# One layer on two batches on one core: which engine makes the low parts, and in what order the last parts are added

## The chip, the cores and the metric

The kernel runs on one core of a Trainium2 chip. The metric is the device time in microseconds (us) of one execution. The engines are TensorE (PE, matmuls), VectorE (DVE), ScalarE (ACT) and GpSimd (POOL), each of which runs its own instructions in order; SyncE (SP) issues the DMAs, in order too. On PE a weight load (PEld) goes ahead of each matmul.

## What is computed

One encoder layer with a final norm, with the same weights, for a batch `x_sample` of 512 tokens and a batch `x_prompt` of 1024 tokens, with 1024 channels, all in float32:

```python
def encoder_layer(x, ...):
    h = rmsnorm(x, g_attn)
    proj = h @ w_in                              # q, k, v of two mixers and the gates
    ...
    a = dilated_mixture(qa, ka, va, rel_bias)    # 3 groups of 4 heads
    a = a.reshape(b, s, A_OUT_WIDTH) @ w_a_out
    bo = window_gqa(qb, kb, vb, rel_bias, sink)  # 8 query heads
    bo = bo @ w_b_out
    g_a, g_b = jnp.split(jax.nn.sigmoid(gates + b_gate), 2, axis=-1)
    x = x + (g_a * a + g_b * bo) @ w_o
    u = dwconv(rmsnorm(x, g_ffn) @ w_up, conv_w, conv_b)
    u_gate, u_val = jnp.split(u, 2, axis=-1)
    return x + (jax.nn.gelu(u_gate) * u_val) @ w_down   # D_FF = 2816

def trunk(x, ...):
    return rmsnorm(encoder_layer(x, ...), g_final)
```

## The kernel before

**Split operands.** Every matmul operand is split into a high part `hi`, cast by ScalarE to a shorter format, and a low part `lo` = value − `hi`, subtracted by VectorE or GpSimd. A product is the sum of three matmuls, hi·hi, hi·lo and lo·hi. So before PE can use a tile, ScalarE casts it and another engine subtracts; the third matmul needs the subtraction. `wload` (L123) does this for weights: a DMA into `raw`, the cast to `whi` (L138), the subtraction to `wlo` (L141), every third weight on VectorE and the others on GpSimd.

**Stages.** The sample runs first: norm, projections and attention, `merge`, `ffn`. In the middle of its `ffn` (after channel tiles 11 and 15) the prompt's norm is mixed in. Then the prompt: attention, `merge`, an up-projection with fewer products (`up_strassen`), and `down`.

**Branch inputs.** `merge` first makes six split inputs `ab` with `branch_in` (L715), two for mixer A, four for mixer B: loads of an attention output `bo` and of a factor row `bf`, their product on VectorE (L730), for mixer A the sum of three of them (L732), the cast `abhi` (L735), the subtraction `ablo` on GpSimd (L736). `bo` and `bf` lie in a pool of as many buffers as there are row tiles (4 in the sample, 8 in the prompt).

**Merge.** For each of 8 channel tiles `j`: the two branches' matmuls into `psa`, multiplied into the gates `sg` on VectorE (L803), added on GpSimd (L806), cast to `mhi` (L807), subtracted to `mlo` on GpSimd (L808). The split tile and its rows of `w_o` form a part. `accumulate` (L822) adds parts to the residual: for each job, that is 128 tokens by 512 channels, three matmuls for each part into one PSUM bank `pacc`, then one addition to `xacc` on VectorE (L835). The last group of the sample has parts 6 and 7, and 8 jobs; that of the prompt parts 6 and 7, and 16 jobs.

**ffn of the sample.** For each of 22 channel tiles `i`, two up-projections with their convs (L861 to L864), GELU, the gated product `y` (L878), its cast `ghi` (L881) and its subtraction `glo` on GpSimd (L882), which with the rows of `w_down` form a part. Every second tile two parts are accumulated. At the end parts 20 and 21 are left; 8 jobs share a pool of four banks. For the first four jobs part 20 goes into four banks with an addition each, then part 21 with another four; for the last four jobs both parts go into one bank.

**down of the prompt.** For each half of the tokens and each of 22 parts `k`, `prepare` (L1102) loads a piece `graw` of the gated product and the weight rows `wraw` into a pool of 6 buffers and splits them with `ring_split` (L986 on) into three pairs of `rhi` and `rlo`, out of a ring of 7 buffers each. Eight banks hold the sums of 4 row tiles by 2 halves of the channels. Parts go one after the other over all banks, but in the second half the last two parts go row tile by row tile: 12 matmuls, then two additions to `xres` (L1154), the final norm, and the output `yo` (L1118), which is stored.

**Order.** Programs of the engines are not in the order of the source: a scheduler places the instructions of each engine in an order of its own by the dependences, so the rows of the order are shown with the change.

## Time and profile before

| | |
|---|---|
| median of three runs | 2279.0 us (2277.1, 2279.0, 2288.47) |
| profiled execution | 2286.05 us |
| its span, first to last instruction | 2284.2 us |
| mean granted clock of PE | 0.983 |
| PE busy | 2189.2 us, 96% of the span |
| VectorE busy | 1273.4 us, 56% |
| ScalarE busy | 1016.6 us, 45% |
| GpSimd busy | 573.7 us, 25% |
| chain that ended last | PE 75%, VectorE 5%, GpSimd 3%, ScalarE 3%, issue 2%, DMA 1% |

The three runs give the time; the profiled execution is one more, with its own time, and all rows come from it. A share of the chain says which engine's work the end of the program goes back to. The granted clock is the share of full speed, 2.4 GHz, that PE's matmuls had; 0.50 is 1.2 GHz.

### The profile page before, as it was taken

To read this page: it belongs to the slowest core of one execution; us is meant where nothing else is said; L and a number is where in the kernel's file an instruction comes from. 1 tells how busy PE (TensorE), PEld (TensorE's weight loads), DVE (VectorE), ACT (ScalarE), POOL (GpSimd) and SP (SyncE) were. 2 spreads that over 40 slices of the span, in tenths; PEclk is the share of its full clock that TensorE was granted. 3 is DMA by queue.
4 is the path that set the end of the run, shared out by engine and by line. 5 is a ranking of instruction groups with operands and counts; after the bars stand their busy time and mean duration, and the time that the engine had idled before them with its cause. 6 is when DMAs were issued, how large, how long until landed. Compare 5 with 4: busy or idle time off the path is not lost.

```text
span 2284.2 us, 28441 instructions
## 1 busy us (share of the span) xinstructions
PE 2189.2 (96%) x10627; PEld 1822.3 (80%) x10627; DVE 1273.4 (56%) x2161; ACT 1016.6 (45%) x1878; POOL 573.7 (25%) x322
## 2 busy tenths in 40 slices
PE   7999999899999999999999999998899999999998
PEld 6877777688878888989787788887778888888886
DVE  4547532554464446465577443434978888863534
ACT  5646532433354336565577212124555555543433
POOL 2211154333333310110000423231733333200000
PEclk9999999899999999999999999999999999999999
DMA  5454353333333331324211921112222222254542
GB/s 168 136 159 125 121 154 105 102 101 94 101 121 100 94 97 47 106 78 128 63 41 54 271 61 45 50 44 96 87 67 83 83 83 83 87 212 140 172 155 101
DMA packets 247981, 240.80 MB, mean 105 GB/s; under 512 B 19808, under 2 KB 204848, under 8 KB 247844
## 3 DMA queue, kind: packets, MB, share of 16 engines
q1 hardware_dynamic: 247844, 238.99, 33.6%
q8 instruction: 83, 1.36, 0.2%
q14 instruction: 54, 0.44, 0.1%
HBM read 202.46 MB, written 42.79 MB: 107 GB/s over the span
## 4 chain that ended last, share of the span: by engine, by line
PE 75%; DVE 5%; POOL 3%; ACT 3%; issue 2%; DMA 1%; SPq 0%; DVEq 0%; ACTq 0%; POOLq 0%
PE psuA L984 9%; PE psuC L984 4%; PE pacc L833 4%; PE psg L147 4%; PE psg L149 3%; PE psg L148 3%; PE pacc L1114 3%; PE pacc L1113 3%; PE pacc L1115 3%; PE pacc L832 3%; PE pacc L831 3%; PE psu L148 3%; PE psu L147 3%; PE psu L149 3%; PE psuB L984 2%
## 5 line engine op out<-in xcount | busy, mean ns | idle before, releaser
L141 POOL TENSOR_TENSOR wlo<-raw,whi 128x1024 fp32r<-128x1024 f32 (+1 forms) x120 | 282.5, 2360 | 869.8 <-ACT whi L138 664.2
L138 ACT CAST whi<-raw 128x1024 fp32r<-128x1024 f32 (+1 forms) x178 | 182.3, 1031 | 381.0 <-PE pacc L833 133.5
L835 DVE TENSOR_TENSOR xacc<-xacc,pacc 128x512 f32<-128x512 f32 x236 | 159.1, 687 | 142.8 <-PE pacc L833 142.2
L141 DVE TENSOR_TENSOR wlo<-raw,whi 128x1024 fp32r<-128x1024 f32 (+1 forms) x58 | 72.6, 1251 | 147.6 <-ACT whi L138 147.4
L147 PE MATMUL psg<-hhi,whi 128*128 128x512 f32 x384 | 151.0, 393 | 1.1 <-ACT frow L520 1.1
L148 PE MATMUL psg<-hlo,whi 128*128 128x512 f32 x384 | 150.5, 392 | 0.0
L149 PE MATMUL psg<-hhi,wlo 128*128 128x512 f32 x384 | 150.4, 392 | 0.0
L990 ACT CAST rhi<-rraw 128x512 fp32r<-128x512 f32 x132 | 81.4, 622 | 139.7 <-PE psuA L984 51.0
L147 PE MATMUL psu<-hhi,whi 128*128 128x512 f32 x352 | 137.6, 391 | 0.0
L149 PE MATMUL psu<-hhi,wlo 128*128 128x512 f32 x352 | 137.3, 390 | 0.0
L148 PE MATMUL psu<-hlo,whi 128*128 128x512 f32 x352 | 137.3, 390 | 0.0
L1114 PE MATMUL pacc<-rlo,rhi 128*128 128x512 f32 x352 | 137.2, 390 | 0.0
L1115 PE MATMUL pacc<-rhi,rlo 128*128 128x512 f32 x352 | 136.9, 389 | 0.0
L1113 PE MATMUL pacc<-rhi 128*128 128x512 f32 x352 | 136.8, 389 | 0.0
L991 DVE TENSOR_TENSOR rlo<-wraw,rhi 128x512 fp32r<-128x512 f32 x88 | 57.3, 689 | 133.3 <-ACT rhi L990 133.3
L991 DVE TENSOR_TENSOR rlo<-rraw,rhi 128x512 fp32r<-128x512 f32 x132 | 108.4, 839 | 23.3 <-ACT rhi L990 21.2
L803 DVE TENSOR_TENSOR sg<-sg,psa 128x512 f32<-128x512 f32 x48 | 32.9, 687 | 152.3 <-PE psa L149 127.5
L990 ACT CAST rhi<-wraw 128x512 fp32r<-128x512 f32 x88 | 50.5, 619 | 148.2 <-PE pacc L1115 144.5
L147 PE MATMUL psq<-hhi,whi 128*128 128x512 f32 x240 | 100.3, 418 | 1.2 <-DVE vb L356 0.7
L148 PE MATMUL psq<-hlo,whi 128*128 128x512 f32 x240 | 96.6, 402 | 0.0
L149 PE MATMUL psq<-hhi,wlo 128*128 128x512 f32 x240 | 96.1, 400 | 0.0
L1019 POOL TENSOR_TENSOR rraw<-rraw 128x512 f32<-128x512 f32 x44 | 89.9, 2044 | 15.7 <-DVE rlo L991 12.7
(254 smaller groups left out, 6108.5 us busy)
## 6 DMA issues: line engine op xcount, KB each, us to landing
raw<-in_w_in_dram SPq DMA_DIRECT2D x80, 512.0 KB
raw<-in_w_up_dram SPq DMA_DIRECT2D x44, 512.0 KB
rraw<-in_w_up_dram SPq DMA_DIRECT2D x44, 512.0 KB
wraw<-in_w_down_dram SPq DMA_DIRECT2D x44, 512.0 KB
raw<-in_w_down_dram SPq DMA_DIRECT2D x22, 512.0 KB
gv<-y SPq DMA_DIRECT2D x22, 512.0 KB
graw<-gv SPq DMA_DIRECT2D x44, 256.0 KB
raw<-in_w_o_dram SPq DMA_DIRECT2D x16, 512.0 KB
```

The lines of the kernel that those rows point to most:

```text
L138: nc.scalar.copy(out=hi[:, :n], in_=raw[:, :n])
L141: eng.tensor_tensor(out=lo[:, :n], in0=raw[:, :n], in1=hi[:, :n].bitcast(F32), op=ALU.subtract)
L147: mm(out, whi, r[0], start=start, stop=False)
L148: mm(out, whi, r[1], start=False, stop=False)
L149: mm(out, wlo, r[0], start=False, stop=stop)
L835: nc.vector.tensor_tensor(out=x, in0=x, in1=p, op=ALU.add)
L984: mm(out, a[:, cols], b, start=start and j == 0 and n == 0, stop=j == 3 and n == 2, skip_group_check=True)
L990: nc.scalar.copy(out=hi, in_=src)
L991: nc.vector.tensor_tensor(out=lo, in0=src, in1=hi.bitcast(F32), op=ALU.subtract)
L1113: mm(p, a, whi, start=first, stop=False)
L1114: mm(p, a, wlo, start=False, stop=False)
L1115: mm(p, b, whi, start=False, stop=last)
```

## The change

Five places are edited.

1. `wload`: while a layer has made at most `quick` weights, the subtraction is on VectorE. `quick` is 0, and 4 in the sample, whose first norm stands at the program's start. The third weight was on VectorE already.
2. `branch_in`: all subtractions `ablo` on VectorE.
3. `merge`: for the last channel tile, the sum and the subtraction on VectorE. `accumulate` with `late=True`, used for the last group (in the prompt for its first 8 of 16 jobs): all parts but the last go into the first four banks ahead of the last part's matmuls.
4. `ffn`: for the last channel tile the subtraction on VectorE; part 20 is accumulated for all 8 jobs with an addition each, and then part 21 for all 8 with another: 16 additions where there were 12.
5. `down`: in the second half the last three parts, 19 to 21, go row tile by row tile, 18 matmuls each, and their pieces `ehi` and `elo` have a pool of their own of 9 buffers each, outside of the ring.

Behind the first edit the line numbers grow by one (`branch_in`, `merge`), and at the end by 22.

```diff
     def __init__(self, tc, w, const, dram):
         self.tc, self.nc, self.w, self.c, self.dram = tc, tc.nc, w, const, dram
-        self.loads = 0
+        self.loads = self.quick = 0
...
     def wload(self, srcs, ncols, pool=None):
...
         nc.scalar.copy(out=hi[:, :n], in_=raw[:, :n])
         self.loads += 1
-        eng = nc.vector if self.loads % 3 == 0 else nc.gpsimd
+        eng = nc.vector if self.loads % 3 == 0 or self.loads <= self.quick else nc.gpsimd
         eng.tensor_tensor(out=lo[:, :n], in0=raw[:, :n], in1=hi[:, :n].bitcast(F32), op=ALU.subtract)
         return hi, lo
...
         self.wden = self.ms.tile([P, self.NT, 8], F32, tag="wden", name="wden")
         if rows is not None:
+            self.quick = 4
             turn = vectors[0](self.qk, "qk")
             for tt in range(0, NT, 2):
...
         hi, lo = (ab.tile([P, T], F32R, tag="ab", name=n) for n in ("abhi", "ablo"))
         nc.scalar.copy(out=hi, in_=acc)
-        nc.gpsimd.tensor_tensor(out=lo, in0=acc, in1=hi.bitcast(F32), op=ALU.subtract)
+        nc.vector.tensor_tensor(out=lo, in0=acc, in1=hi.bitcast(F32), op=ALU.subtract)
         return hi, lo
...
             for hf, cols in enumerate(halves):
                 t = sg[0][hf]
-                nc.gpsimd.tensor_tensor(out=t, in0=t, in1=sg[1][hf], op=ALU.add)
+                eng = nc.vector if j == KT - 1 else nc.gpsimd
+                eng.tensor_tensor(out=t, in0=t, in1=sg[1][hf], op=ALU.add)
                 nc.scalar.copy(out=mhi[:, cols], in_=t)
-                nc.gpsimd.tensor_tensor(out=mlo[:, cols], in0=t, in1=mhi[:, cols].bitcast(F32), op=ALU.subtract)
+                eng.tensor_tensor(out=mlo[:, cols], in0=t, in1=mhi[:, cols].bitcast(F32), op=ALU.subtract)
             merged.append((mhi, mlo, wo))
         if norm is None:
-            self.accumulate(merged, pw, "w")
+            self.accumulate(merged, pw, "w", late=True)
             return
         del self.h
-        self.accumulate(merged, pw, "w", range(0, 4))
+        self.accumulate(merged, pw, "w", range(0, 4), late=True)
         norm = norm(ps, "m")
         next(norm)
...
         return norm
...
-    def accumulate(self, parts, psum, tag, tiles=None):
+    def accumulate(self, parts, psum, tag, tiles=None, late=False):
         nc = self.nc
         mm = nc.tensor.matmul
-        for tt in tiles or range(self.NT):
-            for nh in range(2):
-                cols = slice(nh * 512, nh * 512 + 512)
-                p = psum.tile([P, 512], F32, tag=tag, name="pacc")
-                for i, (hi, lo, (whi, wlo)) in enumerate(parts):
-                    a, b = hi[:, tt * P:(tt + 1) * P], lo[:, tt * P:(tt + 1) * P]
-                    mm(p, a, whi[:, cols], start=i == 0, stop=False)
-                    mm(p, a, wlo[:, cols], start=False, stop=False)
-                    mm(p, b, whi[:, cols], start=False, stop=i == len(parts) - 1)
-                x = self.x[tt][:, cols]
-                nc.vector.tensor_tensor(out=x, in0=x, in1=p, op=ALU.add)
+        def add(p, i, tt, cols):
+            hi, lo, (whi, wlo) = parts[i]
+            a, b = hi[:, tt * P:(tt + 1) * P], lo[:, tt * P:(tt + 1) * P]
+            mm(p, a, whi[:, cols], start=i == 0, stop=False)
+            mm(p, a, wlo[:, cols], start=False, stop=False)
+            mm(p, b, whi[:, cols], start=False, stop=i == len(parts) - 1)
+        jobs = [(tt, slice(nh * 512, nh * 512 + 512)) for tt in tiles or range(self.NT) for nh in range(2)]
+        early = [psum.tile([P, 512], F32, tag=tag, name="pacc") for _ in jobs[:4]] if late else []
+        for p, job in zip(early, jobs):
+            for i in range(len(parts) - 1):
+                add(p, i, *job)
+        for n, (tt, cols) in enumerate(jobs):
+            p = early[n] if n < len(early) else psum.tile([P, 512], F32, tag=tag, name="pacc")
+            for i in range(len(parts) - 1 if n < len(early) else 0, len(parts)):
+                add(p, i, tt, cols)
+            x = self.x[tt][:, cols]
+            nc.vector.tensor_tensor(out=x, in0=x, in1=p, op=ALU.add)
...
     def ffn(self, ctx, hooks, xnp):
...
             lo = gvp.tile([P, T], F32R, tag="glo", name="glo")
             nc.scalar.copy(out=hi, in_=yv)
-            nc.gpsimd.tensor_tensor(out=lo, in0=yv, in1=hi.bitcast(F32), op=ALU.subtract)
+            eng = nc.vector if i == FT - 1 else nc.gpsimd
+            eng.tensor_tensor(out=lo, in0=yv, in1=hi.bitcast(F32), op=ALU.subtract)
             parts.append((hi, lo, self.wload([W["w_down"][i * P:(i + 1) * P, :]], D, wdp)))
             if i in hooks:
                 hooks[i](dn, "d")
             if i == FT - 1:
-                first = range(NT // 2)
-                self.accumulate(parts[:-1], dn, "d", first)
-                self.accumulate(parts[-1:], dn, "d", first)
+                self.accumulate(parts[:-1], dn, "d")
             if i == FT - 2:
                 gf = xnp.tile([P, D], F32, tag=xtag, name="gf")
                 nc.sync.dma_start(gf, bass.AP(tensor=c["g_final"].tensor, offset=c["g_final"].offset,
                                               ap=[[0, P], [1, D]]))
-        self.accumulate(parts, dn, "d", range(NT // 2, NT))
+        self.accumulate(parts[-1:], dn, "d")
         for tt in range(NT):
             y = xnp.tile([P, D], F32, tag=xtag, name="yo")
...
         xp, yo, sm = pool("xres", 8), pool("yo", 4), pool("dsm", 4)
         W = self.w
+        end = pool("end", 9)
         gf = pool("gf", 1).tile([P, D], F32, name="gf")
         gsrc = self.c["g_final"]
         nc.sync.dma_start(gf, bass.AP(tensor=gsrc.tensor, offset=gsrc.offset, ap=[[0, P], [1, D]]))
...
+        def split(src, last):
+            if not last:
+                return self.ring_split(src)
+            hi, lo = (end.tile([P, 512], F32R, tag=f"e{s}", name=f"e{s}") for s in ("hi", "lo"))
+            nc.scalar.copy(out=hi, in_=src)
+            nc.vector.tensor_tensor(out=lo, in0=src, in1=hi.bitcast(F32), op=ALU.subtract)
+            return hi, lo
         def prepare(half, k):
+            last = half == 1 and k >= FT - 3
             graw = self.rraw.tile([P, 512], F32, tag="rraw", name="graw")
             nc.sync.dma_start(graw, self.gv_d[k][:, half * 512:half * 512 + 512])
             wraw = self.rraw.tile([P, D], F32, tag="rraw", name="wraw")
             nc.sync.dma_start(wraw, W["w_down"][k * P:(k + 1) * P, :])
-            return self.ring_split(graw), [self.ring_split(wraw[:, nh * 512:nh * 512 + 512]) for nh in range(2)]
+            return split(graw, last), [split(wraw[:, nh * 512:nh * 512 + 512], last) for nh in range(2)]
...
         def add(w, p, tt, nh, first, last):
...
                 for tt, x in enumerate(xs):
                     nc.sync.dma_start(x, self.x_d[half * 4 + tt])
-            if half == 1 and k == FT - 2:
+            if half == 1 and k >= FT - 3:
                 continue
-            if half == 0 or k < FT - 2:
+            if half == 0 or k < FT - 3:
                 w = ready.pop(0)
                 for tt in range(4):
...
             y = yo.tile([P, D], F32, tag="y", name="yo")
             for nh, cols in enumerate(halves):
-                for i in range(2):
-                    add(ready[i], acc[tt, nh], tt, nh, False, i == 1)
+                for i in range(3):
+                    add(ready[i], acc[tt, nh], tt, nh, False, i == 2)
                 nc.vector.tensor_tensor(out=x[:, cols], in0=x[:, cols], in1=acc[tt, nh], op=ALU.add)
             rs, = self.rstd([x], sm, lambda: y, 2)
...
```

The order of the instructions at three places:

VectorE (DVE) at the sample's last down-projection, before; `y` is the conv's output and then the gated product, `xacc` the residual:

```order
L862 SCALAR_TENSOR_TENSOR y<-psu,vecs,y 128x511
L835 TENSOR_TENSOR xacc<-xacc,pacc 128x512
L864 SCALAR_TENSOR_TENSOR y<-psu,vecs,y 128x511
L835 TENSOR_TENSOR xacc<-xacc,pacc 128x512
L878 TENSOR_TENSOR y<-y 128x512
L835 TENSOR_TENSOR xacc<-xacc,pacc 128x512 x6
L184 RECIPROCAL rs<-rs 128x1
```

and after:

```order
L847 TENSOR_TENSOR xacc<-xacc,pacc 128x512
L876 SCALAR_TENSOR_TENSOR y<-psu,vecs,y 128x511
L847 TENSOR_TENSOR xacc<-xacc,pacc 128x512
L890 TENSOR_TENSOR y<-y 128x512
L847 TENSOR_TENSOR xacc<-xacc,pacc 128x512 x2
L895 TENSOR_TENSOR glo<-y,ghi 128x512
L847 TENSOR_TENSOR xacc<-xacc,pacc 128x512 x11
L184 RECIPROCAL rs<-rs 128x1
```

`glo` of part 21, which GpSimd made, now stands among the additions, and eight additions of each kind (part 20, part 21) stand where six pairs and a joint sum stood.

TensorE (PE) at the same place, before, with numbers since the names differ by them; `whi_6568` is the weight of part 20 and `whi_6652` that of part 21:

```order
L831 MATMUL pacc_6672<-whi_6568,ghi_6563 128x512
L832 MATMUL pacc_6672<-wlo_6569,ghi_6563 128x512
L833 MATMUL pacc_6672<-whi_6568,glo_6564 128x512
L831 MATMUL pacc_6677<-whi_6652,ghi_6647 128x512
L832 MATMUL pacc_6677<-wlo_6653,ghi_6647 128x512
L833 MATMUL pacc_6677<-whi_6652,glo_6648 128x512
```

and after, the same six places:

```order
L833 MATMUL pacc_6672<-whi_6568,ghi_6563 128x512
L834 MATMUL pacc_6672<-wlo_6569,ghi_6563 128x512
L835 MATMUL pacc_6672<-whi_6568,glo_6564 128x512
L833 MATMUL pacc_6677<-whi_6568,ghi_6563 128x512
L834 MATMUL pacc_6677<-wlo_6569,ghi_6563 128x512
L835 MATMUL pacc_6677<-whi_6568,glo_6564 128x512
```

Behind the fourth bank (`pacc_6672`) the next four banks of part 20 follow, where part 21 stood; part 21 begins twelve matmuls later.

VectorE at the prompt's branch inputs, before; `bo` is a branch output times its factor `bf`, `ablo` its low part:

```order
L730 TENSOR_TENSOR bo<-bo,bf 128x1024 x2
L732 TENSOR_TENSOR bo<-bo 128x1024
L141 TENSOR_TENSOR wlo<-raw,whi 128x1024
L730 TENSOR_TENSOR bo<-bo,bf 128x1024
L732 TENSOR_TENSOR bo<-bo 128x1024
L730 TENSOR_TENSOR bo<-bo,bf 128x1024 x2
L803 TENSOR_TENSOR sg<-sg,psa 128x512 x2
L730 TENSOR_TENSOR bo<-bo,bf 128x1024 x2
L803 TENSOR_TENSOR sg<-sg,psa 128x512 x2
```

and after:

```order
L731 TENSOR_TENSOR bo<-bo,bf 128x1024
L733 TENSOR_TENSOR bo<-bo 128x1024
L737 TENSOR_TENSOR ablo<-bo,abhi 128x1024
L731 TENSOR_TENSOR bo<-bo,bf 128x1024
L737 TENSOR_TENSOR ablo<-bo,abhi 128x1024
L731 TENSOR_TENSOR bo<-bo,bf 128x1024
L804 TENSOR_TENSOR sg<-sg,psa 128x512 x2
L737 TENSOR_TENSOR ablo<-bo,abhi 128x1024
L731 TENSOR_TENSOR bo<-bo,bf 128x1024
L737 TENSOR_TENSOR ablo<-bo,abhi 128x1024
L731 TENSOR_TENSOR bo<-bo,bf 128x1024
L737 TENSOR_TENSOR ablo<-bo,abhi 128x1024
```

A subtraction follows each product, and the one of the fourth input stands behind two gate products (`sg`).

ScalarE (ACT) at the prompt's last weights, before:

```order
L990 CAST rhi<-graw 128x512
L990 CAST rhi<-wraw 128x512 x2
L990 CAST rhi<-graw 128x512
L990 CAST rhi<-wraw 128x512 x2
L179 ACTIVATE yo,ms<-xres 128x512
```

and after; `ehi` are the pieces of parts 19 to 21:

```order
L1119 CAST ehi<-graw 128x512
L1119 CAST ehi<-wraw 128x512
L1001 CAST rhi<-wraw 128x512 x2
L1001 CAST rhi<-graw 128x512
L1119 CAST ehi<-wraw 128x512
L1119 CAST ehi<-graw 128x512
L1119 CAST ehi<-wraw 128x512 x2
L1119 CAST ehi<-graw 128x512
L1001 CAST rhi<-wraw 128x512 x2
L1119 CAST ehi<-wraw 128x512 x2
L179 ACTIVATE yo,ms<-xres 128x512
```

The casts of parts 19 to 21 stand among, and in part ahead of, those of parts 17 and 18.

## Rows read from the trace of the kernel before

**Rows 1.** PE's waits over the span: what waited for what, us in total, times, longest

```profile
PE pacc L831 <- ACT ghi L881: 4.7, 2, 3.6
PE psa L148 <- POOL ablo L736: 4.1, 4, 1.7
PE pacc L833 <- POOL mlo L808: 3.3, 5, 1.2
PE psv L305 <- POOL wlo L141: 1.6, 1, 1.6
```

**Rows 2.** windows: length, busy us (count) of PE, PEld, DVE, ACT, POOL; PEclk; DMA

```profile
297.60:301.00 3.40, 3.40 (x10) 2.63 (x9) 0.37 (x1) 0.42 (x1) 1.28 (x1) 0.50 0.62 218
813.10:819.80 6.70, 6.08 (x13) 4.29 (x14) 2.64 (x5) 2.45 (x4) 1.27 (x1) 0.50 0.01 2
819.90:825.30 5.40, 5.36 (x24) 4.07 (x22) 4.41 (x14) 3.40 (x8) 0.00 (x0) 1.00 0.00 0
```

**Rows 3.** timeline at the sample's last down-projection: start, us, engine, line, instruction, idle before

```profile
812.81 0.68 DVE L835 TENSOR_TENSOR xacc<-xacc,pacc 128x512 f32<-128x512 f32 x1
812.93 0.62 ACT L881 CAST ghi<-y 128x512 fp32r<-128x512 f32 x1 [4.11 <-DVE y L878]
813.60 0.80 PE L831 MATMUL pacc<-whi,ghi 128*128 128x512 f32 x1 [3.64 <-ACT ghi L881]
813.62 1.27 POOL L882 TENSOR_TENSOR glo<-y,ghi 128x512 fp32r<-128x512 f32 x1 [8.48 <-ACT ghi L881]
824.87 0.39 PE L833 MATMUL pacc<-whi,glo 128*128 128x512 f32 x1
```

**Rows 4.** timeline of the sample's branch inputs: PE, POOL, DVE and DMA issues

```profile
292.99 1.56 DVE L730 TENSOR_TENSOR bo<-bo,bf 128x512 f32<-128x512 f32 x1 [2.75 <-DMA bf<-frow]
295.26 0.50 PE L147 MATMUL psa<-abhi,whi 128*128 128x512 f32 x1 [1.23 <-ACT abhi L735]
295.29 1.54 POOL L736 TENSOR_TENSOR ablo<-bo,abhi 128x512 fp32r<-128x512 f32 x1 [1.28 <-ACT abhi L735]
296.85 1.09 SPq L728 DMA_DIRECT2D bf<-frow  x2
296.88 0.50 PE L148 MATMUL psa<-ablo,whi 128*128 128x512 f32 x1 [0.88 <-POOL ablo L736]
300.63 0.69 DVE L730 TENSOR_TENSOR bo<-bo,bf 128x512 f32<-128x512 f32 x1 [3.26 <-DMA bf<-frow]
```

**Rows 5.** timeline of the prompt's branch inputs

```profile
1287.42 1.22 DVE L730 TENSOR_TENSOR bo<-bo,bf 128x1024 f32<-128x1024 f32 x1
1299.12 2.18 ACT L735 CAST abhi<-bo 128x1024 fp32r<-128x1024 f32 x2 [3.59 <-DVE bo L730]
1300.24 2.36 POOL L736 TENSOR_TENSOR ablo<-bo,abhi 128x1024 fp32r<-128x1024 f32 x1 [2.24 <-ACT abhi L735]
1302.66 0.50 PE L148 MATMUL psa<-ablo,whi 128*128 128x512 f32 x1 [1.70 <-POOL ablo L736]
```

**Rows 6.** timeline at the last channel tiles of the two merges

```profile
419.19 2.26 POOL L806 TENSOR_TENSOR sg<-sg 128x512 f32<-128x512 f32 x1
422.15 0.50 PE L831 MATMUL pacc<-whi,mhi 128*128 128x512 f32 x1 [0.98 <-ACT mhi L807]
1566.50 0.50 PE L833 MATMUL pacc<-whi,mlo 128*128 128x512 f32 x1 [0.41 <-POOL mlo L808]
```

**Rows 7.** timeline of the first matmuls

```profile
12.65 2.90 DVE L200 TENSOR_SCALAR xin<-xin,rs 128x1024 f32<-128x1024 f32 x1
12.65 5.13 POOL L141 TENSOR_TENSOR wlo<-raw,whi 128x1024 fp32r<-128x1024 f32 x2 [10.88 <-ACT whi L138]
```

**Rows 8.** timeline of the prompt's last row tiles

```profile
2248.17 0.33 SPq L1106 DMA_DIRECT2D wraw<-in_w_down_dram  x1
2273.80 0.39 PE L1115 MATMUL pacc<-rhi,rlo 128*128 128x512 f32 x1
2279.61 1.42 DVE L1118 SCALAR_TENSOR_TENSOR yo<-xres,rs,gf 128x512 f32<-128x512 f32 x2
```

## The prediction

> **What bounds the kernel now.** I read the busy times first: TensorE (PE) works for 96% of the span, so a change that leaves its matmuls alone can win only where PE stands still or runs at the lower clock. Next I read PE's waits, grouped by what ended them [rows 1]: the last product `ghi` of a group 4.7 us, the branch low parts `ablo` 4.1, the merged low parts `mlo` 3.3, the first weight's low part `wlo` 1.6. That is 13.7 us of 2284, and it is the stock that this change draws on. Last I read the granted clock by windows [rows 2]: right after such waits PE runs at 0.50, the 1.2 GHz level, for 6.7 us at 813.1 and for 3.4 us at 297.6. In the window behind the first of them 24 matmuls take 5.4 us, 0.226 us each. The ten that are recorded in the second stretch would need 2.3 of its 3.4 us, which leaves 1.1 lost; half of its length, by the ratio of the clocks, is 1.7. A few records can be missing from a trace, so I count 1.7.
>
> The sum is made against the profiled execution, 2286.05 us (span 2284.2, so 1.85 us lie outside). The median of the runs is 2279.0, 7 us less, and that gap is not explained by anything below; I carry the difference over to the median.
>
> **Part by part.** Negative is a gain.
>
> *a. Start, three weight halves to VectorE: 0 (−1.5 to +1.5).* PE waits 1.6 us for GpSimd's first `wlo` [rows 1], and the normalising instruction on VectorE takes 2.90 us beside GpSimd's two halves of 5.13 us together [rows 7]. With GpSimd out of the way that instruction should shrink, and the transposes that follow it come sooner. But the first `wlo` now queues on VectorE behind two pairs of `hlo` and a second `xin`: 12.65 plus about 4.5 us, so its matmul starts near 17.2 instead of 15.05, with eight transposes done before it that came after. Idle time about equal.
>
> *b1. Sample, branch inputs: −3.0 (−3.6 to −2.0 if all holds, 0 if a later wait takes it).* The step is a ring: product on VectorE, high part on ScalarE, low part on GpSimd, which frees the buffer for the load of the input after next. The load at 296.85 is issued 0.02 us after the GpSimd subtraction (295.29 + 1.54 = 296.83) ends, and the product at 300.63 waits 3.26 us for it [rows 4]. On VectorE the subtraction costs 0.69, as that product does: 0.85 saved in each turn. So not only PE's wait of 0.88 for `ablo` goes; the wait of 1.23 for `abhi` before it and the load after it move up too. Step by step: inputs 2 and 3 come 0.5 to 0.9 us earlier, the subtraction of input 3 ends near 295.1 instead of 296.83 (a weight half of 1.2 us stands ahead of it on VectorE), its matmul starts near 295.2 instead of 296.88, a gain of 1.7. Less idle time there should leave the clock up: 1.7 more. The load then caps the gain: if it did not move, input 5 would be ready at 302, where PE used it at 304.1, a cap of 2.0; since it moves by 1.7, the cap is 3.6. I take 3.0.
>
> *b2. Prompt, branch inputs: +0.5 (−1 to +3).* Here the subtraction takes 2.36 on GpSimd and would take 1.22 on VectorE [rows 5]. But VectorE now runs product and subtraction in turn, as the rows of the order behind the diff show, and each subtraction waits for ScalarE's cast of 1.09 (2.18 for two). A turn is 1.22 + 1.09 + 1.22 = 3.5 us, and the product of input 5 is queued behind the subtraction of input 4, where before it ran ahead. From 1298.5 on (the subtraction of input 3 now stands behind two gate products) the last `ablo` ends at 1305.6; GpSimd ended it at 1300.24 + 2 × 2.36 = 1304.96. PE waits 1.70 for the first of these two today; that falls, and the last one is later by 0.6. The upper end adds a stretch of low clock like the one in [rows 2].
>
> *c. Sample, last channel tile: −1.4 (−1.4 to −0.4).* GpSimd's addition takes 2.26 us and PE then waits 0.98 for the cast [rows 6], and shortly after another 0.4 for the low part, which is in the `mlo` line of [rows 1]. On VectorE the pair costs 2 × 0.69. "Other parts first" gives nothing here, since the scheduler had issued part 6 ahead of part 7 already.
>
> *d. Prompt, last channel tile: −0.4* for the wait at 1566.50 [rows 6]. Nothing else there waits.
>
> *e. Sample, last down-projection: −4.7 (−5.0 to −2.0).* Before, PE stops after 12 matmuls of part 20, at 813.60 − 3.64 = 809.96, until the cast of part 21 (812.93 + 0.62) has ended, and is done with 36 more at 824.87 + 0.39 = 825.26 [rows 3]: 15.3 us, of which 36 × 0.226 = 8.1 is work at full clock. After, all 24 matmuls of part 20 come first. The 12 extra ones need banks that the four additions free; the last of these ends at 812.81 + 0.68 = 813.49, so PE runs until 814.2 with three short waits of about 0.6. By then `ghi` is there (813.55). `glo` on VectorE costs 0.69 behind one addition, ready near 814.9, against 813.62 + 1.27 = 814.89: equal. PE waits 0.3 for it and does the other 24 by 820.2 at full clock: −5.0. Four more additions, 16 instead of 12, cost 0.69 each on VectorE, at a pace (0.61 from start to start) just below PE's 0.68 for a bank; I take 0.3 for them. If the short waits still bring the low clock, about 3 us come back: −2.0.
>
> *f. Prompt, three token-major rows: −1.3 (−2.4 to 0).* PE ends at 2273.80 + 0.39 = 2274.19 and the last output is computed at 2279.61 + 1.42 = 2281.03 [rows 8]: 6.84 us, because VectorE needs about 3.8 us for a row tile (two additions of 0.69, an output of 1.3, eight small ones) where PE needs 12 × 0.226 = 2.7. With 18 matmuls PE needs 4.1 and VectorE keeps up; what is left is the last tile's own chain and one output ahead of it, 5.5 us.
>
> The moved DMA issues cost nothing by what I can see: the sample's outputs go behind loads of the next stage's bias on SP, and nobody waits for an output; the load of the final gain goes later, and its first use is the prompt's first output.
>
> Sum: 0 − 3.0 + 0.5 − 1.4 − 0.4 − 4.7 − 1.3 = −10.3, so 2275.8 for a profiled execution and **2268.7** for the median.
>
> **A rule against the change.** A VectorE instruction that stood beside GpSimd's weight halves took 2.90 us [rows 7], and a product 1.56 where 0.69 is usual [rows 4]. So moved work is not simply 0.69 wherever GpSimd still splits weights. The Trainium skill, SBUF — State Buffer, section Who interferes with whom, says that a VectorE instruction with two SBUF inputs and a GpSimd instruction that reads SBUF exclude each other, the second waiting for the whole of the first. With that rule both rows agree, and applied to each of three places it gives 2276.4 (rival 3) against the 2268.7 of the sum.
>
> **Rivals.** *1. The clock stays up everywhere.* b1 −3.6, c −1.4, d −0.4, e −5.0, f −2.4, b2 −1: −13.8, 2265.2. For it: both stretches follow idle time that shrinks. Against: PE keeps some waits in each place.
> *2. The low clock stays at the ffn end and in the branch inputs.* e −2.0, b1 −1.7, b2 +0.5, the rest as above: −6.3, 2272.7. For it: after the change PE still stops three or four times around 811 to 815.
> *3. GpSimd blocks the moved work.* A half is 5.13 / 2 = 2.57 us; in three places (start, sample branch inputs, sample merge) a moved instruction waits for a whole one: +7.7, so −2.6, 2276.4. Against: GpSimd loses 22 instructions, and in the prompt's branch inputs it has hardly anything else.
> *4. Slower: the casts of the last rows wait for loads.* ScalarE now casts parts 19 to 21 ahead of the weight of part 18, in order, and these casts wait for loads. A weight is issued at 2248.17 [rows 8] and the DMA engines are quiet by 2251, so 2.9 us. With that, part 18 is split about 1.2 us before PE wants it, and part 21 about 2.4 before. With a landing of L us PE waits (L − 4.1) + (L − 5.3): from L = 9.9 on this passes 10.3 with the low clock's share left out. At L = 11 it gives +12.6 − 10.3 = +2.3, 2281.3. Nothing at this place in the trace is that slow.
>
> **Chances.** Forecast (−8 to −12.5) 0.45; rival 1 0.30; rival 2 0.13; rival 3 0.08; rival 4 0.04. A measurement can tell about 0.5%, 11.4 us: faster than 2267.6 holds rival 1 and the better edge of the forecast, 0.38; slower than 2290.4 asks for L of about 15.6 in rival 4, or for something I do not see, 0.02; same 0.60. The range leaves out the far ends of rivals 1 and 3, and rival 4: 2263 to 2277.
>
> **What would show it.** In the changed profile: PE's wait for `ghi` at the sample's last group falls from 3.6 to under 0.5 and the first matmul of the prompt's values comes 5 us sooner after the group began; no window at 0.50 within 15 us of it (rival 2 if there is). In the sample's branch inputs no wait for `ablo` above 0.3, and the last load issued 1.5 us earlier; in the prompt's a wait for `abhi` above 1 us appears. The end lies 5.5 us behind the last matmul. Any PE wait for `ehi`, `elo` or `rhi` after 2230 is rival 4. I would be wrong if a place that was not edited changes by more than 2 us.

## The result

The changed kernel takes 2269.3 us (median of 7 runs, 2262.4 to 2270.6) against 2279.0 of the kernel before (7 runs, 2276.7 to 2288.5): ratio 0.995, 95% interval 0.9936 to 0.9964, a gain of 8 to 15 us. In a second series, beside a further kernel, it took 2265.7 against 2279.7, ratio 0.9941 (0.9928 to 0.9955). 2268.7 was forecast, with a range of 2263 to 2277.

The profiled execution fell by more, from 2286.05 to 2270.56, because that of before was a long one. So a term must not be read off this pair alone; the experiments below give more profiles of each place with its edit, and for all places but the last down-projection also several without.

**The page after**, part 1, answers to the table of before: GpSimd (POOL) works 51.5 us less, VectorE (DVE) 15.8 more, and PE is busy 8 us less with the same 10,627 matmuls. Up to its last matmul PE stands at 0.50 for 47.8 us where it was 71.7, which fits that. Little of it can be put down to the edits: the eleven other profiles below have 34 to 61 us, and ffn_engine, which is the kernel before with one subtraction moved, has 44.

```profile
PE 2181.1 (96%) x10627; PEld 1815.7 (80%) x10627; DVE 1289.2 (57%) x2187; ACT 1016.4 (45%) x1878; POOL 522.2 (23%) x300
```

**PE's waits over the span** of the changed kernel, as in [rows 1] (what waited for what, us in total, times, longest):

```profile
PE psa L147 <- ACT abhi L736: 4.6, 4, 1.5
PE pacc L835 <- POOL mlo L810: 3.2, 3, 1.2
PE psa L148 <- DVE ablo L737: 1.3, 3, 0.5
PE pacc L833 <- ACT ghi L893: 1.0, 1, 1.0
PE pacc L833 <- DVE xacc L847: 1.0, 3, 0.5
PE psv L305 <- DVE wlo L141: 0.8, 1, 0.8
```

The 3.6 us for `ghi` are gone (the 1.0 left is from another part), `ablo` fell from 4.1 to 1.3 but the cast `abhi` ahead of it rose, from 3.3 in the view of before (in a further profile of the changed kernel, after_again, it is 3.6), and a new wait of 1.0 stands for the additions that free the banks.

**The sample's last down-projection**, timeline, where [rows 3] showed the wait of 3.64 (start, us, engine, line, instruction, idle before):

```profile
800.92 0.50 PE L833 MATMUL pacc<-whi,ghi 128*128 128x512 f32 x1 [0.45 <-DVE xacc L847]
...
802.76 0.62 ACT L893 CAST ghi<-y 128x512 fp32r<-128x512 f32 x1 [4.11 <-DVE y L890]
803.38 0.50 PE L833 MATMUL pacc<-whi,ghi 128*128 128x512 f32 x1 [0.24 <-DVE xacc L847]
803.84 0.69 DVE L895 TENSOR_TENSOR glo<-y,ghi 128x512 fp32r<-128x512 f32 x1
809.85 0.39 PE L835 MATMUL pacc<-whi,glo 128*128 128x512 f32 x1
```

The cast waits just as long as before (4.11 behind `y`), but PE no longer waits for it: it fills the time with part 20, with three short stops for banks. The window at that place and the one behind it stay at full clock (columns as in [rows 2]):

```profile
797.00:804.00 7.00, 6.02 (x25) 4.00 (x23) 6.21 (x10) 2.27 (x3) 0.00 (x0) 1.00 0.44 128
804.00:811.00 7.00, 6.59 (x29) 4.83 (x28) 7.00 (x12) 3.43 (x5) 0.41 (x2) 1.00 0.14 38
```

**The sample's branch inputs**, timeline, for [rows 4]:

```profile
286.26 2.40 POOL L141 TENSOR_TENSOR wlo<-raw,whi 128x1024 fp32r<-128x1024 f32 x1 [11.57 <-ACT whi L138]
287.48 1.73 DVE L731 TENSOR_TENSOR bo<-bo,bf 128x512 f32<-128x512 f32 x1 [0.92 <-DMA bf<-frow]
289.92 0.50 PE L147 MATMUL psa<-abhi,whi 128*128 128x512 f32 x1 [1.53 <-ACT abhi L736]
290.27 0.68 DVE L737 TENSOR_TENSOR ablo<-bo,abhi 128x512 fp32r<-128x512 f32 x1
290.98 1.09 SPq L729 DMA_DIRECT2D bf<-frow  x2
291.19 0.40 PE L148 MATMUL psa<-ablo,whi 128*128 128x512 f32 x1
```

and the window behind it, which is at full clock where [rows 2] had 0.50:

```profile
291.20:294.60 3.40, 3.40 (x16) 2.59 (x15) 1.13 (x3) 0.62 (x1) 0.00 (x0) 1.00 0.71 225
```

The load is again issued 0.03 us after the subtraction ends, now VectorE's (290.27 + 0.68). PE has no wait at `ablo` of this input, the fourth of six; the wait for its cast is 1.53.

**The prompt's branch inputs**, PE's waits in the timeline, for [rows 5]:

```profile
1285.18 0.73 PE L147 MATMUL psa<-abhi,whi 128*128 128x512 f32 x2 [1.02 <-ACT abhi L736]
1286.44 0.50 PE L148 MATMUL psa<-ablo,whi 128*128 128x512 f32 x1 [0.53 <-DVE ablo L737]
1288.65 0.73 PE L147 MATMUL psa<-abhi,whi 128*128 128x512 f32 x2 [1.02 <-ACT abhi L736]
1289.91 0.50 PE L148 MATMUL psa<-ablo,whi 128*128 128x512 f32 x1 [0.53 <-DVE ablo L737]
```

Four waits, 3.1 us, where there were 0.50, 1.70 and 0.69: the turn of product, cast and subtraction is what PE waits for, twice.

**The end**, VectorE and PE, for [rows 8]:

```profile
2260.10 0.39 PE L1137 MATMUL pacc<-ehi,elo 128*128 128x512 f32 x1
2261.70 1.28 DVE L1140 SCALAR_TENSOR_TENSOR yo<-xres,rs,gf 128x1024 f32<-128x1024 f32 x1
2264.43 1.41 DVE L1140 SCALAR_TENSOR_TENSOR yo<-xres,rs,gf 128x512 f32<-128x512 f32 x2
```

From 2260.49 to 2265.84 it is 5.35 us, where it was 6.84.

### The profile page after: what moved, and what is told of

The parts are those of the page before. It is cut to its first block, busy times and chain, and to the rows that moved or that the text cites. A ratio compares the mean times of both kernels' runs of the same rounds, so it can differ in the third digit from the quotient of the medians.

```text
span 2268.8 us, 28430 instructions
## 1 busy us (share of the span) xinstructions
PE 2181.1 (96%) x10627; PEld 1815.7 (80%) x10627; DVE 1289.2 (57%) x2187; ACT 1016.4 (45%) x1878; POOL 522.2 (23%) x300
## 4 chain that ended last, share of the span: by engine, by line
PE 76%; DVE 5%; issue 3%; ACT 2%; DMA 1%; POOL 1%; SPq 0%; DVEq 0%; ACTq 0%; POOLq 0%
PE psuA L995 10%; PE psuC L995 5%; PE pacc L835 4%; PE pacc L1136 3%; PE pacc L1137 3%; PE pacc L1135 3%; PE pacc L834 3%; PE pacc L833 3%; PE psu L149 3%; PE psu L147 3%; PE psu L148 3%; PE psg L149 3%; PE psg L148 3%; PE psg L147 3%; PE psuB L995 2%
## 5 line engine op out<-in xcount | busy, mean ns | idle before, releaser
L141 POOL TENSOR_TENSOR wlo<-raw,whi 128x1024 fp32r<-128x1024 f32 (+1 forms) x117 | 274.6, 2353 | 903.8 <-ACT whi L138 709.2
L1136 PE MATMUL pacc<-rlo,rhi 128*128 128x512 f32 x328 | 127.7, 389 | 0.0
L1137 PE MATMUL pacc<-rhi,rlo 128*128 128x512 f32 x328 | 127.6, 389 | 0.0
L1135 PE MATMUL pacc<-rhi 128*128 128x512 f32 x328 | 127.4, 389 | 0.0
L1002 DVE TENSOR_TENSOR rlo<-rraw,rhi 128x512 fp32r<-128x512 f32 x132 | 106.2, 821 | 26.4 <-ACT rhi L1001 24.3
L414 DVE TENSOR_TENSOR ptlo<-pst,pthi 128x512 fp32r<-128x512 f32 (+1 forms) x128 | 82.6, 654 | 14.2 <-ACT pthi L413 12.8
```

The source lines that it names most:

```text
L141: eng.tensor_tensor(out=lo[:, :n], in0=raw[:, :n], in1=hi[:, :n].bitcast(F32), op=ALU.subtract)
L1002: nc.vector.tensor_tensor(out=lo, in0=src, in1=hi.bitcast(F32), op=ALU.subtract)
L1135: mm(p, a, whi, start=first, stop=False)
L1136: mm(p, a, wlo, start=False, stop=False)
L1137: mm(p, b, whi, start=False, stop=last)
```

## The experiments

All matmul counts are equal, so a place can be measured in every trace by the same two matmuls outside of it: the table gives the time from the start of the k-th to that of the m-th recorded matmul (us), and for the end from the start of the last one to the end of the span. Bold is where the run has that place's edit, or one beyond it.

| profile | start 0–240 | sample branch inputs 1380–1460 | sample last tile 1900–1980 | ffn end 3570–3710 | prompt branch inputs 6380–6480 | prompt last tile 7380–7600 | end |
|---|---|---|---|---|---|---|---|
| before | 58.3 | 25.6 | 21.6 | 36.3 | 32.6 | 50.6 | 10.4 |
| ffn_only | 54.7 | 24.8 | 21.6 | **31.7** | 31.9 | 50.6 | 10.4 |
| ffn_order | 55.5 | 22.9 | 21.6 | **31.3** | 31.9 | 50.6 | 10.4 |
| ffn_engine | 55.6 | 23.9 | 21.6 | 34.5 | 31.7 | 50.6 | 10.4 |
| changed | **57.8** | **21.9** | **19.7** | **31.7** | **32.6** | **49.9** | **8.7** |
| after_again | **58.4** | **20.6** | **19.6** | **31.7** | **32.5** | **49.9** | **8.7** |
| branch_pool | **58.0** | 24.3 | **19.6** | **31.7** | 32.6 | **49.9** | **8.7** |
| branch_mixed | **59.1** | **20.4** | **19.7** | **31.7** | 32.1 | **49.9** | **8.7** |
| no_quick | 57.0 | **21.3** | **19.6** | **31.7** | **32.3** | **49.9** | **8.7** |
| tail4 | **57.8** | **20.3** | **19.7** | **31.7** | **33.0** | **49.9** | **7.8** |
| merge_all | **57.7** | **20.4** | **18.3** | **31.7** | **31.8** | **49.9** | **8.7** |
| best | 58.0 | **21.9** | **18.3** | **31.7** | **32.2** | **49.9** | **8.7** |
| best4 | 55.4 | **20.3** | **18.3** | **31.7** | **32.9** | **49.9** | **7.8** |

Three columns hold stretches at 0.50 besides the edit: the start one of 3.4 or 6.8 us from 55 us on in ten of the thirteen profiles, the sample's branch inputs one of 3.4 in four of the five without the edit, the prompt's branch inputs 3.4 to 10.2 us in all.

My theory was the prediction's sum, place by place. Its rival was that the median had moved by the clock's steps in places without an edit.

**The ffn end, both edits, the order alone, the engine alone**, each on the kernel before:

```diff
             if i == FT - 1:
-                first = range(NT // 2)
-                self.accumulate(parts[:-1], dn, "d", first)
-                self.accumulate(parts[-1:], dn, "d", first)
+                self.accumulate(parts[:-1], dn, "d")
...
-        self.accumulate(parts, dn, "d", range(NT // 2, NT))
+        self.accumulate(parts[-1:], dn, "d")
```

```diff
-            nc.gpsimd.tensor_tensor(out=lo, in0=yv, in1=hi.bitcast(F32), op=ALU.subtract)
+            eng = nc.vector if i == FT - 1 else nc.gpsimd
+            eng.tensor_tensor(out=lo, in0=yv, in1=hi.bitcast(F32), op=ALU.subtract)
```

ffn_only (both). 

> The kernel before with the fourth edit alone (order of the last down-projection of the sample, 16 additions, low part on VectorE). My theory: the place from the first matmul of part 20 to the first matmul of the prompt's values takes about 13.5 us instead of 18.2, that is 4.7 less, and the median falls by 4 to 6 us against before, about half of the whole change. Rival (the change's gain is the clock's, not the edit's): the place shrinks, but the median moves by under 2 us since stretches of low clock appear elsewhere.

ffn_order (the first diff). 

> The kernel before with the order of the last down-projection alone; the low part of part 21 stays on GpSimd. My theory: the order alone does it, since the low part on GpSimd is ready at about the same time (1.27 us from the cast's end at 813.55, so 814.9) as on VectorE (0.69 us, but behind an addition); the place takes 13.5 to 14 us, within 0.5 of the run with both. Rival: the low part on VectorE is needed; here PE waits 0.5 us or more for it and the clock falls, place 15 us or more.

ffn_engine (the second). 

> The kernel before with the low part of part 21 on VectorE and the old order. My theory: the wait of 3.6 us for the high part stays, so does the low clock after it; the place takes 17.5 to 18.2 us instead of 18.2. Rival: the engine is what matters, 15 us or less.

Measured: ffn_only 2273.9 against 2281.1, ratio 0.9965 (0.9952 to 0.9977); ffn_order 2273.1, ratio 0.9976 (0.9963 to 0.999); ffn_engine one run, 2272.8, which says nothing about 2 us. The first two medians fell by 7.2 and 7.9 us, more than the place and more than the 4 to 6 that I expected; the runs of one kernel are spread over 4 to 12 us here. The place is 4.6 us shorter with both and 5.0 with the order alone. The low part of part 21 on GpSimd came when it was needed: in the timeline of ffn_order it ends at 806.58 + 1.30 = 807.88, and PE's first use, at 807.94, comes only 0.16 us later than an unbroken row of matmuls would have had it.

```profile
806.58 1.30 POOL L882 TENSOR_TENSOR glo<-y,ghi 128x512 fp32r<-128x512 f32 x1 [8.48 <-ACT ghi L881]
807.55 0.40 PE L832 MATMUL pacc<-wlo,ghi 128*128 128x512 f32 x1
807.94 0.50 PE L833 MATMUL pacc<-whi,glo 128*128 128x512 f32 x1
```

With the engine alone the wait stays. The place is 1.8 us shorter there, where I expected at most 0.7; the stretch of low clock is 3.4 us long where before had 6.8, and half of the difference is 1.7. The timeline, and a window:

```profile
804.98 0.79 PE L831 MATMUL pacc<-whi,ghi 128*128 128x512 f32 x1 [3.64 <-ACT ghi L881]
```

```profile
804.60:808.00 3.40, 3.02 (x7) 2.40 (x8) 1.71 (x4) 0.32 (x1) 0.00 (x0) 0.50 0.02 5
```

So the order is what gains here. The engine gains nothing and costs a little: with `glo` on VectorE the additions behind it come later. In the changed kernel and ffn_only PE starts the second job of part 21 0.30 us late for its bank, and waits 0.31 us for the last addition at its next stage. In ffn_order these are 0.11 and 0.10, and the place takes 31.3 us where all others with the edit take 31.7.

```profile
810.55 0.39 PE L304 MATMUL psv<-whi,hhi 128*128 128x256 f32 x1 [0.31 <-DVE xacc L847]
```

**Branch inputs back on GpSimd**, in both batches, and in the prompt alone:

```diff
-        nc.vector.tensor_tensor(out=lo, in0=acc, in1=hi.bitcast(F32), op=ALU.subtract)
+        nc.gpsimd.tensor_tensor(out=lo, in0=acc, in1=hi.bitcast(F32), op=ALU.subtract)
```

```diff
+        (nc.vector if T == 512 else nc.gpsimd).tensor_tensor(out=lo, in0=acc, in1=hi.bitcast(F32), op=ALU.subtract)
```

branch_pool. 

> The changed kernel with the low parts of the branch inputs back on GpSimd in both batches. My theory: the stretch of the sample's branch inputs takes 3 to 4 us longer than in the changed kernel (27.5 to 28 us between the matmuls that are 24.2 apart there), with waits for the low part of 0.9 and with the load of the last input issued at the end of GpSimd's subtraction; the prompt's is the same within 1 us; the median rises by 3 to 4 us against the changed kernel. Rival: only PE's two waits for the low part come back (1.7 us), because the loads do not hang on the subtraction.

branch_mixed. 

> The changed kernel with the low parts of the branch inputs on VectorE in the sample and on GpSimd in the prompt. Theory: in the sample as in the changed kernel (no wait for a low part above 0.3), in the prompt the waits of before (0.5 for abhi, 1.7 and 0.7 for ablo, 2.3 for mhi), so that the two stretches differ from the changed kernel by under 1 us in sum at equal clock. Rival: GpSimd is better in the prompt by over 1 us, since the changed kernel's waits there are 6.2 us in sum against 5.4.

Measured: the sample's place takes 24.3 us in branch_pool, which has GpSimd, and 20.3 to 21.9 in eight profiles with VectorE (mean 20.9); the five profiles without the edit have 22.9 to 25.6 (mean 24.3). In the waits of branch_pool the two for GpSimd's low part are back, and the window behind them is at 0.50 again:

```profile
PE psa L147 <- ACT abhi L736: 1.7, 2, 1.2
PE psa L148 <- POOL ablo L737: 1.7, 2, 0.9
```

```profile
291.80:295.20 3.40, 3.40 (x10) 2.62 (x9) 0.14 (x2) 0.62 (x1) 1.27 (x1) 0.50 0.59 202
```

The prompt's place is 32.3 to 33.0 with VectorE (four profiles in which nothing else there differs, mean 32.6) and 31.7 to 32.6 with GpSimd (six, mean 32.2). The two overlap, so the half microsecond between them is not clear of the stretches of low clock. The median of branch_pool, 2269.0 (ratio 0.995, 0.9934 to 0.9967), does not rise by the 3 to 4 us that I expected: its runs lie 10 us apart, those of the changed kernel 8, and the medians cannot tell this part. branch_mixed is one run, 2270.4.

**The first edit taken back:**

```diff
-            self.quick = 4
```

no_quick. 

> The changed kernel without the first edit: the first weights' low parts stay on GpSimd. From the runs so far the first 240 matmuls take 57.8 and 58.0 us with the edit, and 54.7, 55.5, 55.6 and, in the profile of before, 58.3 without it; the clock comes up at 21.9 and 22.2 with it, at 18.4, 18.7 and 21.1 without. Theory: the edit costs 1 to 2.5 us at the start, since PE is kept waiting until later and comes up to full clock later; here the first 240 matmuls take 55 to 56.5 us and the median is 1 to 2 us below the changed kernel. Rival (what was predicted): the edit is worth nothing either way; 57 to 58.5 us here too, and what differed between the runs was where the clock's steps happened to fall.

Measured: 57.0 us for the first 240 matmuls, at the rival's edge, and 2265.9 (ratio 0.9935, 0.9917 to 0.9952). Over all profiles it is 57.7 to 59.1 with the edit (six, mean 58.1) and 54.7 to 58.3 without (seven, mean 56.4): 1.8 us on average, the two overlap. What does not overlap is where PE reaches its full pace. PE's last wait before its unbroken row, with the edit (changed kernel) and without (no_quick):

```profile
17.26 0.58 PE L305 MATMUL psv<-wlo,hhi 128*128 128x256 f32 x1 [0.77 <-DVE wlo L141]
```

```profile
15.03 0.58 PE L305 MATMUL psv<-wlo,hhi 128*128 128x256 f32 x1 [1.64 <-POOL wlo L141]
```

and one window of the changed kernel and of ffn_order, the same 3.5 us, busy throughout:

```profile
18.40:21.90 3.50, 3.50 (x18) 3.50 (x17) 3.14 (x5) 1.05 (x3) 0.00 (x0) 1.00 0.86 241
```

```profile
18.40:21.90 3.50, 3.50 (x30) 3.33 (x30) 3.04 (x7) 1.71 (x5) 0.00 (x0) 1.00 0.57 164
```

18 matmuls against 30: the granted clock printed here is not to be trusted, since no step of the clock is recorded yet; the count shows it. The first recorded step up lies at 21.5 to 22.6 in the six profiles with the edit and at 18.4 to 21.1 in the seven without. By matmul 220, ahead of the stretch at 0.50 from 55 us on, the edit has cost 1.0 us (50.8 against 49.9 on average). The rest of the 1.8 is that stretch, which all six profiles with the edit have and four of the seven without; whether the edit brings it on is open. So the edit has a cost of 1 to 2 us, not a gain.

**All channel tiles of both merges on VectorE:**

```diff
-                eng = nc.vector if j == KT - 1 else nc.gpsimd
+                eng = nc.vector
```

merge_all. 

> The changed kernel with sum and low part of every channel tile of both merges on VectorE, not only of the last. Theory (the waits for GpSimd's sum and low part are what the merges lose, wherever they stand): PE's waits for mhi and mlo in the sample (1.6, 1.1 and 1.2 us) and at the prompt's first tile (2.3 and 0.8) fall by 4 to 5 us in sum, and with them a stretch of low clock or two: 4 to 7 us less than the changed kernel over the two merges. Rival: VectorE, in order, takes on 44 pairs of 1.4 us, its products for PE come later, and the merges get longer by 1 us or more.

Measured: 2261.8, ratio 0.992 (0.9899 to 0.9941). In the sample's last two groups PE waits, in the changed kernel and then in merge_all:

```profile
PE pacc L835 <- POOL mlo L810: 2.3, 2, 1.2
PE pacc L833 <- ACT mhi L809: 1.6, 1, 1.6
```

```profile
PE pacc L833 <- ACT mhi L809: 1.5, 1, 1.5
```

Only the waits for the low part go; 1.3 us in the last tile and 1.1 in the group ahead of it (8.8 where profiles without a stretch of low clock there have 9.7 to 10.0). The wait for the cast stays, since the cast is queued on ScalarE behind a weight's, which waits for its load. In the prompt 2.3 for the cast and 0.8 for the low part became 2.0 for the cast. The waits fell by 3.5 us in sum, where I expected 4 to 5. VectorE did not become the bound.

**Four row-major parts at the end:**

```diff
-        end = pool("end", 9)
+        end = pool("end", 12)
...
-            last = half == 1 and k >= FT - 3
+            last = half == 1 and k >= FT - 4
```

and the two other places that name the three parts. tail4. 

> The changed kernel with four parts (18 to 21) row tile by row tile, 24 matmuls each, and an end pool of 12. Theory: with 18 matmuls (4.1 us) PE already takes longer for a row tile than VectorE (3.8), so four parts give nothing more: the last output ends 5.2 to 5.5 us behind PE's last matmul, as in the changed kernel (5.35), and PE has no wait for the pieces. Rival: VectorE was still behind with three, and the end comes 0.7 us or more nearer (4.6 or less).

Measured: the rival's number, in one run (2267.5). The last output ends at 2261.43 + 1.41 = 2262.84, 4.46 us behind PE's last matmul at 2257.99 + 0.39; no wait for a piece appears.

```profile
2256.48 1.28 DVE L1140 SCALAR_TENSOR_TENSOR yo<-xres,rs,gf 128x1024 f32<-128x1024 f32 x1
2257.99 0.39 PE L1137 MATMUL pacc<-ehi,elo 128*128 128x512 f32 x1
2261.43 1.41 DVE L1140 SCALAR_TENSOR_TENSOR yo<-xres,rs,gf 128x512 f32<-128x512 f32 x2
```

The output of the third row tile now runs before PE's last matmul instead of between the last addition and the last tile's chain. Three parts had not removed VectorE's lag: of 6.84 us they took 1.5, the fourth 0.9 more.

**The changed kernel again, and versions that put these together:** best is the changed kernel without `quick` and with merge_all's edit, best4 has tail4's as well.

after_again. 

> The changed kernel once more, beside the next kernel on the same chip, and with a further profile of it. By the places (start +1 to +2.5, sample branch inputs -2.4 to -5, sample merge -2.0, ffn end -4.6, prompt merge -0.7, tail -1.7, prompt branch inputs 0) the edits sum to -8.5 to -11.5 us; ratio 0.995 to 0.996. Rival: the first verdict was helped by the clock's steps in the places without an edit, and the ratio is above 0.997.

best. 

> The changed kernel without its first edit and with sum and low part of every channel tile on VectorE in both merges. By the two runs that did one of these each (about 1.5 and 4 to 5 us by their places) it takes 5 to 7 us less than the changed kernel on the same chip. Rival: the two do not add, since the start's difference is only where the clock's steps fall; then it takes 3 to 4.5 us less.

best4. 

> The changed kernel without its first edit, with sum and low part of every channel tile of both merges on VectorE, and with four parts row tile by row tile at the end. Theory: the 0.9 us at the end come on top of what the kernel without the four parts gained (2262.0 against 2265.7 of the changed kernel on one chip): about 4.5 us under the changed kernel, ratio to before about 0.9915. From PE's last matmul's start to the end of the span 7.8 us. Rival: the median doesn't show it, since the places without an edit differ by more than 0.9 from run to run; the stretch behind the last matmul is 7.8 all the same.

Measured: after_again 2265.7 and best 2262.0 on one chip, ratios 0.9941 and 0.9918 (0.9904 to 0.9932); best4 2261.5 on another, 0.9929 (0.9911 to 0.9946). after_again gained more than the ratio of 0.995 to 0.996 that I expected, and so did not bear out its rival. best is 3.7 us under the changed kernel beside it, the rival's number and not the 5 to 7 that I expected, and the two intervals still touch. By their ratios merge_all, best and best4 lie 3 to 7 us under the changed kernel, and they cannot be told from each other. For best4 this is the rival too: the end's 0.9 stands in the place (7.8) but not in the median, and neither does the start's 1 to 2 us.

## Why the prediction was right

The sum of the terms as the profiles now show them, with the mean where there are several, is +1.8 − 3.4 + 0.5 − 2.0 − 0.7 − 4.6 − 1.9 = −10.3, the same as the sum that was forecast. That they agree to the tenth is luck: the start was missed by +1.8 and the ffn end by +0.1, and b1, c, d and f by −0.4, −0.6, −0.3 and −0.6. What was right is the mechanism of the larger terms, the waits that went and the places where PE kept its clock. (With the mean of two profiles for the ffn end, below, it is −9.4.)

- **a, start:** forecast 0 (±1.5), measured +1.8 on average. The idle time was equal, as worked out (0.64 and 1.64 before; 0.64, 0.53, 0.36 and 0.77 after), and the matmul started at 17.26 for 17.2. The instruction beside GpSimd's halves shrank as forecast, from 2.90 to 0.75. What the term left out is that PE is at half speed there and comes up only after its unbroken row has begun, which is now 2.2 us later.
- **b1, sample's branch inputs:** forecast −3.0, measured −3.4. The wait for `ablo` went, and the clock stayed up. ffn_order, the one profile without the edit that has no stretch of low clock there, takes 22.9 us, 2.0 above the mean with the edit; so some 2 us are waits and the rest is the clock, near the 1.7 and 1.7 of the prediction. The ring through the load was right: the issue is 0.03 us behind the subtraction, and counted from matmul 1380 it comes 1.4 us earlier on average (17.3 to 18.9 us with the edit, 18.6 to 20.4 without), for the 1.5 forecast. But it did not cap the gain: apart from 0.44 us in ffn_order, PE waits for the third and fourth input alone, with the edit and without it. The product of the fourth still took 1.73 us beside a weight half of GpSimd, 1.56 before, and the wait for its cast is still 1.53. The spread of 20.3 to 21.9 goes by the third: PE waits 1.0 us for its cast in the changed kernel and in best, which take 21.9, 0.4 in no_quick and not at all in the other five.
- **b2, prompt's:** forecast +0.5, measured +0.5, with the forecast wait for `abhi` of 1.0, twice. The size is not clear of the spread, as said above.
- **c and d, last channel tiles:** forecast −1.4 and −0.4, measured −2.0 and −0.7. The mis-sized step is what a wait costs. In the trace of before two waits of 0.98 and 0.40 were counted by their idle time:

```profile
422.15 0.50 PE L831 MATMUL pacc<-whi,mhi 128*128 128x512 f32 x1 [0.98 <-ACT mhi L807]
422.48 0.39 PE L832 MATMUL pacc<-wlo,mhi 128*128 128x512 f32 x1
422.71 0.40 PE L831 MATMUL pacc<-whi,mhi 128*128 128x512 f32 x1
423.51 0.50 PE L833 MATMUL pacc<-whi,mlo 128*128 128x512 f32 x1 [0.40 <-POOL mlo L808]
423.85 0.40 PE L832 MATMUL pacc<-wlo,mhi 128*128 128x512 f32 x1
```

  From 422.71 to 423.51 it is 0.80 where an unbroken row has 0.226, and from 423.51 to 423.85 it is 0.34: the idle time of 0.40 cost 0.57 + 0.11, 0.69 before rounding. Of the 0.28 beyond the idle time 0.17 is how the profile counts, since a matmul is shown with 0.40 and the next one starts after 0.226; 0.11 is the slow start behind the wait. Two such waits are 1.38 + 2 × 0.28 = 1.9, and the one of d is 0.69. That "other parts first" changes nothing in the sample was read from the order and was not run apart, nor was what order and engine each do in the prompt.
- **e, ffn end:** forecast −4.7, measured −4.6, with three waits for banks of 0.45, 0.29 and 0.24, for the 0.6 each that were forecast, no delay at `glo`, 0.30 for the bank behind it, and 0.31 at the end. Before's 36.3 is one profile with 6.7 us of low clock; ffn_engine, with the same wait, had 34.5, so the gain is 2.8 to 4.6 by where the clock's step falls.
- **f, end:** forecast −1.3, measured −1.9. Like for like, from the last matmul to the last output, it is −1.5 (5.35 us, where 5.5 was forecast); 0.3 more lie behind the last output, and 0.15 ahead of the last matmul. "VectorE keeps up" was too strong, as tail4 shows.

Of the rivals: the clock did stay up at both places, as in rival 1, but the forecast's −3.0 and −4.7 count on that too. Its −13.8 is not the first series' −9.7, but it is near the second's −14.0; the sum by places lies between, and the two series cannot say which is nearer. Rival 2's window at 0.50 did not come. Rival 3: GpSimd does hold up VectorE, but mostly the products that it held up before too. Of the moved instructions in the branch inputs and the last tiles two were stretched, a subtraction to 1.45 us from 1.23 and the sum of the sample's last tile to 1.39 from 0.69, and PE waited for neither. Rival 4: PE has no wait between 2200 us and its last matmul, with three parts or with four.

A place without an edit did change by more than 2 us, which I had named as a sign of being wrong. From matmul 1280 to 1320 of the sample's attention, before and then the changed kernel, with the same instructions:

```profile
250.40:262.90 12.50, 11.44 (x42) 8.92 (x42) 2.91 (x5) 4.09 (x5) 1.84 (x1) 0.75 0.34 106
```

```profile
248.30:258.50 10.20, 9.04 (x43) 7.28 (x42) 2.99 (x4) 4.08 (x5) 1.82 (x1) 1.00 0.41 129
```

ffn_order and best, with the same code there, took 12.4 and 12.5 us, the others 10.2. In the pair of profiles the edited places sum to −13.2 us and all others to −2.3, which together are the 15.5 of the spans.

## What to carry to other kernels

Where PE waits for the last part of a sum, give it the other parts of all sums first. What the engine of the low part is worth hangs on the place: nothing at the ffn end, 2 to 3.4 us in the sample's branch inputs, 1.3 and 1.1 in merge_all's two groups. Count a short wait of PE as its idle time in the profile plus a quarter of a microsecond, and look behind it for a stretch of low clock. Measure an edit at its place, between two matmuls outside of it, in several profiles: the intervals of the medians here are 6 to 10 us wide. The ffn end and the last tiles repeat to 0.1 us with the same edit; the start and the branch inputs, with their stretches of low clock and products held up, only to 1 or 2.

## What the runs showed of the hardware

**A stop costs more than its idle time.** The matmul behind a wait is followed after 0.34 us instead of 0.226, as in the timeline of c and d above. So it is in 18 of the 19 waits above 0.2 us that stand among such matmuls at full clock in the changed kernel's trace.

**The clock also falls behind small waits.** In merge_all, behind waits of 1.1 and 0.7 us for an earlier part of the sample's ffn, a stretch at 0.50 stands that the changed kernel's profile does not have; from matmul 2060 to 3570 it is 340.8 us in merge_all and 339.0 in the changed kernel.

```profile
PE pacc L833 <- ACT ghi L893: 1.1, 1, 1.1
PE pacc L835 <- POOL glo L895: 0.7, 1, 0.7
```

```profile
663.50:666.80 3.30, 3.30 (x9) 2.53 (x9) 2.13 (x4) 0.00 (x0) 1.77 (x1) 0.50 0.06 16
```

The same two waits, 0.8 to 1.2 and 0.7 us, stand in all thirteen profiles; the clock falls behind them in three, merge_all, no_quick and best. Why it falls in one execution and not in another stays open; no run here was made for it.

**VectorE waits for the whole of a GpSimd instruction.** Beside GpSimd's half of 286.26 + 2.40 = 288.66 the product begun at 287.48 ends at 289.21, 0.55 us after it, which is nearly its own 0.69. In the sample's last tile of the changed kernel it is the same with a moved sum, 413.56 against GpSimd's 413.01:

```profile
411.74 1.27 POOL L810 TENSOR_TENSOR mlo<-sg,mhi 128x512 fp32r<-128x512 f32 x1
412.17 1.39 DVE L808 TENSOR_TENSOR sg<-sg 128x512 f32<-128x512 f32 x1
```

It holds through the trace of the changed kernel. Of the 58 VectorE `TENSOR_TENSOR` instructions with two inputs of 128x512 in SBUF that begin inside one of GpSimd's, 53 end 0.55 us behind its end. The other five run at their usual time inside two GpSimd instructions, of 1.84 and 4.09 us, which began together with VectorE's work or in the middle of it. Those with an input in PSUM, such as the additions to `xacc`, keep their usual 0.67 to 0.69. The Trainium skill, SBUF — State Buffer, section Who interferes with whom, has this as a lock for the length of an instruction, and these rows agree. One row that the prediction counted under that rule is of another kind: the instruction of 2.90 us is a `TENSOR_SCALAR` with one tensor as input. It too ended 0.55 us behind GpSimd's first half.

Moving work to VectorE did not take these waits away. Counted as what such instructions took beyond 0.69 or 1.22 us (an estimate from their usual times), VectorE was held up for 63 us before, 62 in the changed kernel and 72 in merge_all, where the moved sums and low parts themselves wait behind weight halves. Most of it stands in the prompt's up-projection, which no edit touches. So the risk that the prediction weighed is real; in these places it did not reach PE.
